# Squares of the second x tile by halves, its scaling in three pieces, the meta rows on GpSimd: the first normalization of a hybrid decoder layer

## The chip, the cores and the metric

The kernel runs on one core of one Trainium2 chip. A core has five engines, each with its own instruction queue: TensorE (PE, matrix products; PEld is its weight load), VectorE (DVE), ScalarE (ACT), GpSimd (POOL) and SyncE (SP, which here only issues DMAs). They run independently and wait for each other by semaphores. Data lie in SBUF (128 partitions) and products in PSUM, which is read by VectorE and ScalarE alone. The metric is the device time of one execution in microseconds (us), the median over several runs.

## The reference

One layer of a Hymba-like decoder on 1024 positions of width 1024, in float32, with 16 learned meta rows in front:

```python
meta = jnp.broadcast_to(meta_tokens[None].astype(x.dtype), (bsz, N_META, D_MODEL))
h = jnp.concatenate([meta, x], axis=1)
...
    u = rmsnorm(h, g_pre_mix[l])
    z = u @ w_in[l]
    q, k, v, xr, yr = jnp.split(z, split_at, axis=-1)
    attn = sliding_window_attention_with_sinks(...)
    xr = causal_depthwise_conv(xr, conv_w[l], conv_b[l])
    hr = rg_lru(xr, w_a[l], b_a[l], w_x[l], b_x[l], lru_lambda[l])
    rec = (jax.nn.gelu(yr.astype(jnp.float32)) * hr).astype(h.dtype)
    mix = jnp.concatenate([attn.astype(h.dtype), rec], axis=-1) @ w_out[l]
    h = h + rmsnorm(mix, g_post_mix[l])
    u = rmsnorm(h, g_pre_ffn[l])
    f = jnp.square(jax.nn.relu(u @ w_ff1[l])) @ w_ff2[l]
    h = h + rmsnorm(f, g_post_ffn[l])
return h[:, N_META:]
```

`rmsnorm` divides a row by the root of its mean square plus 1e-6 and multiplies it by a gain. Here only the first of these matters, `u = rmsnorm(h, g_pre_mix)`, and of it only the first 272 rows: 16 meta rows and two tiles of x with 128 rows each.

## The kernel before

Every product is made of three: each operand is split into a rounded high part and a low rest, and high*high, high*low and low*high are summed in PSUM. The high part is written by ScalarE (a copy that rounds), the low part by VectorE (a subtraction).

The beginning goes in blocks of rows: block 0 has the meta rows and x tiles 0 and 1, blocks 1 to 3 two tiles of x each. For block 0:

1. Eleven idle products (line 339) keep TensorE busy from the start while the first DMAs arrive (meta rows by ScalarE's queue; x tiles 0 and 1, the gain and the key weights by SP's).
2. Each row's sum of squares is taken: of the meta rows by ScalarE (260); of tile 0 in halves, columns 0 to 511 by ScalarE (235) and 512 to 1023 by VectorE (242, a custom instruction and the reading of its accumulator); of tile 1 by ScalarE alone (235, 1024 columns).
3. The reciprocal root: of tiles 0 and 1 by ScalarE's square root (82) and VectorE's reciprocal (195); of the meta rows by two GpSimd operations (166 and 172).
4. The rows are scaled by it on VectorE: tile 0 in two halves (248), the meta rows (266), tile 1 in two halves (248), in this order.
5. TensorE transposes them, eight column blocks kc of 128. For kc 0 to 5 (line 401) it turns all of tile 0 first, then the gain column (into a bank of its own, copied by ScalarE, 415), then the meta rows, then tile 1; kc 6 and 7 (line 426) come between the first products.
6. For each kc, ScalarE multiplies the bank by the gain and rounds it (117, the eviction), VectorE makes the low rest (118), and TensorE starts the key projection (309): first the high parts in the order of the kc, then the low ones. The products of values and queries follow, and from there TensorE has work until the end of the program.

The order on an engine is that in which a scheduler puts the code; around here it is tied by hand. `behind(name, ins)` puts an instruction after the one named, on the same engine, without a wait; `scaled[0]` holds the name of VectorE's last scaling, `last_lut[0]` of ScalarE's last table function, and `chained(0, ...)` and `chained(1, ...)` keep ScalarE's and VectorE's own chains (`last`). In `transposed_first`, `turn` chains TensorE's transposes in the order of the code.

Of the kernel before, what the change touches and what calls it, by code (L numbers as in the profile page):

```python
# [11 lines left out]
AF = mybir.ActivationFunctionType  # L12
ALU = mybir.AluOpType
# [3 lines left out]
P = 128  # L17
D = 1024
KC = D // P
T = 1024  # L20
NMETA = 16
# [6 lines left out]
EPS = 1e-6  # L28
# [9 lines left out]
def hybrid_layer(  # L38
# [6 lines left out]
    nc = tc.nc  # L45
    x, out = x[0], out[0]
# [11 lines left out]
    def slot(tag, shape, dt=F32):  # L58
        uid[0] += 1
        return slab.tile(shape, dt, tag=tag, name=f"{tag}{uid[0]}", bufs=bufs[tag])  # L60
# [4 lines left out]
    def bank(tag, shape=(P, 512)):  # L65
        uid[0] += 1
        return ps.tile(list(shape), F32, tag=tag, name=f"ps_{tag}{uid[0]}")
# [11 lines left out]
    last_lut = [None]  # L79

    def lut(*args, **kwargs):
        ins = nc.scalar.activation(*args, **kwargs).ins
        if last_lut[0] is not None:
            tc.add_manual_dep(
                ins, last_lut[0],
                mybir.DependencyInfo(
                    mybir.DependencyClass.NoSync, mybir.DependencyReason.DATA
                ),
                reason="lut",
            )  # L90
        last_lut[0] = ins.name
        return ins
# [48 lines left out]
    meta_t = slot("d", [NMETA, D])  # L141
    nc.scalar.dma_start(meta_t, meta_tokens)
    xt = []
# [19 lines left out]
    def rstd_of(ssq_parts, n=P):  # L163
        ms = small.tile([P, 1], F32, name="ms", tag="ms")
        if len(ssq_parts) == 1:
            nc.gpsimd.tensor_scalar(ms[:n], ssq_parts[0], EPS, None, op0=ALU.add)
        else:
            nc.vector.scalar_tensor_tensor(
                ms[:n], ssq_parts[0], EPS, ssq_parts[1], op0=ALU.add, op1=ALU.add
            )  # L170
        rs = small.tile([P, 1], F32, name="rs", tag="rs")
        last_pow[0] = nc.gpsimd.tensor_tensor(
            rs[:n], ms[:n], half_pow[:n], op=ALU.pow
        ).ins.name
        return rs[:n]
# [4 lines left out]
    eps_col = const.tile([P, 1], F32, name="eps_col")  # L180
# [10 lines left out]
    def root_rstd(ssq, bias, after=None):  # L191
        sd = small.tile([P, 1], F32, name="sd", tag="sd")
        lut(sd, ssq, AF.Sqrt, bias=bias)
        rs = small.tile([P, 1], F32, name="rs", tag="rs")
        ins = nc.vector.reciprocal(rs, sd).ins
        if after:
            behind(after, ins)
        return rs


    def load_cols(cols, tag="ws"):
        raw = slot("raw", [P, KC, P])
        o = 0
        for c0, n in cols:
            w, lo = c0
            nc.sync.dma_start(
                raw[:, :, o : o + n],
                w[:, lo : lo + n].rearrange("(k p) c -> p k c", p=P),
            )
            o += n  # L210
        hi, lo_ = pair(tag, [P, KC, P])
        split(hi, lo_, raw)
        return hi, lo_
# [13 lines left out]
    u = [pair("a", [P, TT]) for _ in range(KC)]  # L227
    RMS_SC = 1.0 / math.sqrt(D)

    def norm_first(src, halves):  # L230

        xn = slot("d", [P, D])
        ss = [small.tile([P, 1], F32, name=f"hq{i}", tag=f"hq{i}") for i in range(2)]
        c = slice(0, 512 if halves else D)
        square = nc.scalar.activation(
            xn[:, c], src[:, c], AF.Square, scale=RMS_SC, accum_out=ss[0]
        ).ins
        if not halves:
            behind(last_lut[0], square)
        if halves:  # L240
            c = slice(512, D)
            nc.vector.tensor_tensor_reduce(
                out=xn[:, c], in0=src[:, c], in1=src[:, c], scale=RMS_SC * RMS_SC,
                scalar=EPS, op0=ALU.mult, op1=ALU.add, accum_out=ss[1],
            )
        rs = root_rstd(ss[0], ss[1] if halves else eps_col, scaled[0])
        for c in (slice(0, 512), slice(512, D)):
            ins = nc.vector.tensor_scalar(
                xn[:, c], src[:, c], rs, None, op0=ALU.mult
            ).ins  # L250
        scaled[0] = ins.name
        return xn

    scaled = [None]


    def norm_meta():
        xn = slot("d", [P, D])
        ssq = small.tile([P, 1], F32, name="ssq", tag="ssq")
        nc.scalar.activation(  # L260
            xn[:NMETA], meta_t[:NMETA], AF.Square, scale=RMS_SC, accum_out=ssq[:NMETA]
        )
        rs = rstd_of([ssq[:NMETA]], NMETA)

        def scale():
            ins = nc.vector.tensor_scalar(
                xn[:NMETA], meta_t[:NMETA], rs, None, op0=ALU.mult
            ).ins
            behind(scaled[0], ins)
            scaled[0] = ins.name  # L270

        return xn, scale

    def norm_rows(src, link, after=None):
        xn = slot("d", [P, D])
        ssq = small.tile([P, 1], F32, name="ssq", tag="ssq")
        ins = nc.scalar.activation(
            xn, src, AF.Square, scale=RMS_SC, accum_out=ssq
        ).ins
        if link:  # L280
            chained(0, ins)
        rs = rstd_of([ssq])
        ins = [nc.vector.tensor_scalar(xn, src, rs, None, op0=ALU.mult).ins]
        if after:
            behind(after, *ins)
        elif link:
            for i in ins:
                chained(1, i)
        scaled[0] = ins[0].name
        return xn  # L290
# [57 lines left out]

    def normed(b):
        if b == 0:  # L350
            xm, scale = norm_meta()
            first = norm_first(xt[0], True)
            scale()
            return [(xm, NMETA), (first, P), (norm_first(xt[1], False), P)]
        after = mark[0]
        rows = [(norm_rows(xt[2 * b + i], b == 2, after), P) for i in range(2)]
        scaled.append(scaled[0])
        return rows


    last = [None, None]

    def chained(e, ins):
        if last[e] is not None:
            behind(last[e], ins)
        last[e] = ins.name
# [29 lines left out]
    def transposed_first(xn):  # L396
        (xm, _), (xa, _), (xb, _) = xn
        n, order = ALL[0][1], [None]

        def turn(dst, src):  # L400
            ins = nc.tensor.transpose(dst, src, ident[: src.shape[0], : src.shape[0]]).ins
            if order[0]:
                behind(order[0], ins)
            order[0] = ins.name

        def cols(kc):
            return slice(kc * P, (kc + 1) * P)

        pts = []
        for kc in range(6):  # L410
            pts.append(bank(("o", "s", "pt")[kc % 3]))
            turn(pts[kc][:, NMETA : NMETA + P], xa[:, cols(kc)])
        pg = bank("acc")
        turn(pg[:, :8], g_r)
        chained(0, nc.scalar.copy(g_mix_col, pg[:, :8]).ins)
        for kc in range(6):
            turn(pts[kc][:, :NMETA], xm[:NMETA, cols(kc)])
        for kc in range(KC):
            if kc < 6:
                pt = pts[kc]  # L420
                turn(pt[:, NMETA + P : n], xb[:, cols(kc)])
            else:
                pt = bank(("o", "s")[kc - 6])
                o = 0
                for x_, m in xn:
                    nc.tensor.transpose(pt[:, o : o + m], x_[:m, cols(kc)], ident[:m, :m])
                    o += m
            uh, ul = u[kc]
            high = split_scaled(
                uh[:, :n], ul[:, :n], pt[:, :n], g_mix_col[:, kc : kc + 1]  # L430
            )
            chained(0, high[0])
            chained(1, high[1])
            mark[0] = high[1].name
# [12 lines left out]
    def split_w(raw, tag="ws"):  # L447
        hi, lo_ = pair(tag, [P, KC, P])
        split(hi, lo_, raw)
        return hi, lo_  # L450

    xn = normed(0)
    last[0] = last_lut[0]
    rk = fetch([(K_COL, P)], pieces=2)
    rv = fetch([(V_COL, P)])
    rq = fetch([(Q_COL, HD), (Q_COL + 4 * HD, HD)], "e")
# [7 lines left out]
    last[1] = scaled[0]  # L464
    chained(1, nc.vector.tensor_copy(wk[0][:, 4:8], rk[:, 4:8]).ins)
    transposed_first(xn)
    low_w(wk, rk)
    wv = high_w(rv, "b")
# [90 lines left out]
    for b in range(4):  # L559
# [3 lines left out]
        if b == 0:  # L563
# [5 lines left out]
            xn = [(norm_rows(xt[2], True), P)]  # L569
# [29 lines left out]
    for c in range(NLRU):  # L599
# [16 lines left out]
        out=above, in_=above, pattern=[[1, P]], compare_op=ALU.is_gt, fill=0.0, base=0,  # L616
# [941 lines left out]
    halves = {}  # L1558
# [159 lines left out]
```

## Time and profile before

| | |
|---|---|
| median of 3 runs | 945.62 us (945.26 to 947.6) |
| profiled execution, its own time | 945.83 us |
| span of it, first to last instruction | 944.1 us |
| TensorE busy | 935.1 us (99%) |
| VectorE, ScalarE, GpSimd busy | 663.2, 505.8, 135.3 us |
| HBM over the span | 143 GB/s |
| granted TensorE clock, mean | 0.999 |

A row of the timeline reads: start in us from the span's beginning, duration in us, engine, line of the kernel, operation, what it writes <- what it reads (buffer numbers left out), shapes, and how many instructions the row merges; in brackets the idle time before it and what ended it. `d` are the normalized rows, `c` the loaded x tiles, `ps_o`, `ps_s`, `ps_pt` and `ps_acc` are PSUM banks, `a` the transposed and split rows, `rs` and `sd` reciprocal root and root, `hq` and `ssq` sums of squares. Instructions of an engine overlap a little, so a duration can reach past the next start. A row of the table by stretches gives, for each engine, the busy time in it and the number of its instructions. In the chain of waits each row is a piece of the path that ended last.

### The profile page before, as it was taken

The numbers are of one execution on the slowest core, as the hardware profiler recorded it, in microseconds if no ns is written. First come the engines' busy times: TensorE is split into PE (matmuls) and PEld (weight loads), VectorE is DVE, ScalarE is ACT, GpSimd is POOL, SyncE is SP. The second block draws the span as 40 slices with busy tenths as digits, with TensorE's granted clock in tenths as the row PEclk, the third lists the DMA queues.
The fourth block names the chain that finished last, engine by engine and source line by source line (L and its number), as shares of the span: only waits on it lengthen the run. The fifth ranks groups of instructions, "written<-read, shape, count | busy, mean of one in ns | idle before, by whom it ended". The sixth has DMA issues, their size and how long they took to land.

```text
span 944.1 us, 12155 instructions
## 1 busy us (share of the span) xinstructions
PE 935.1 (99%) x4562; PEld 780.9 (83%) x4562; DVE 663.2 (70%) x844; ACT 505.8 (54%) x847; POOL 135.3 (14%) x205
## 2 busy tenths in 40 slices
PE   9999999999999999999999999999999999999997
PEld 7999999877888878878888888888888888888885
DVE  7668788789877986755544465477667676779883
ACT  8546765679434854443655575653533443445441
POOL 4104437430021200110000000001121000001201
PEclk9999999999999999999999999999999999999999
DMA  8220011104359768573422374334887756637924
GB/s 274 58 67 23 24 46 45 45 23 146 100 182 290 228 193 287 181 249 129 157 89 90 115 219 119 105 112 114 199 173 173 211 180 190 192 131 208 242 63 90
DMA packets 99622, 135.96 MB, mean 144 GB/s; under 512 B 24358, under 2 KB 63286, under 8 KB 99564
## 3 DMA queue, kind: packets, MB, share of 16 engines
q1 hardware_dynamic: 90220, 109.62, 36.7%
q0 software_dynamic: 8880, 24.19, 12.3%
q10 hardware_dynamic: 464, 1.38, 0.4%
q8 instruction: 36, 0.59, 0.3%
q14 instruction: 22, 0.18, 0.1%
HBM read 113.08 MB, written 21.50 MB: 143 GB/s over the span
## 4 chain that ended last, share of the span: by engine, by line
PE 98%; DVE 1%; DMA 0%; ACT 0%; issue 0%; DVEq 0%; ACTq 0%
PE ps_acc L125 11%; PE ps_acc L130 11%; PE ps_acc L131 11%; PE ps_pt L130 7%; PE ps_pt L125 7%; PE ps_pt L131 7%; PE ps_s L125 6%; PE ps_s L131 6%; PE ps_s L130 6%; PE ps_o L125 5%; PE ps_o L130 5%; PE ps_o L131 5%; PE ps_o L763 2%; PE ps_acc L988 1%; PE ps_acc L309 1%; PE ps_s L693 1%
## 5 line engine op out<-in xcount | busy, mean ns | idle before, releaser
L99 DVE TENSOR_TENSOR ws<-raw,ws 128x1024 fp32r<-128x1024 f32 (+1 forms) x69 | 83.1, 1204 | 73.0 <-PE ps_o L130 23.0
L96 ACT CAST ws<-raw 128x1024 fp32r<-128x1024 f32 (+1 forms) x68 | 69.8, 1026 | 82.9 <-PE ps_o L130 32.8
L96 ACT CAST ws<-e 128x1024 fp32r<-128x1024 f32 x41 | 43.0, 1049 | 85.0 <-PE ps_o L130 37.8
L99 DVE TENSOR_TENSOR b<-b,b 128x1024 fp32r<-128x1024 f32 (+1 forms) x49 | 57.6, 1176 | 27.1 <-PE ps_o L130 21.9
L130 PE MATMUL ps_acc<-a,ws 128*128 128x512 f32 (+3 forms) x224 | 76.3, 341 | 0.0
L125 PE MATMUL ps_acc<-a,ws 128*128 128x512 f32 (+3 forms) x224 | 76.3, 341 | 0.0
L131 PE MATMUL ps_acc<-a,ws 128*128 128x512 f32 (+3 forms) x224 | 75.7, 338 | 0.0
L99 DVE TENSOR_TENSOR ws<-e,ws 128x1024 fp32r<-128x1024 f32 x41 | 50.1, 1223 | 31.4 <-ACT ws L96 18.0
L96 ACT CAST b<-b 128x1024 fp32r<-128x1024 f32 (+1 forms) x49 | 49.6, 1012 | 41.4 <-DVE b L1188 35.3
L750 POOL TENSOR_SCALAR_AFFINE_SELECT c<-c 128x512 fp32r<-128x512 f32 x64 | 53.1, 844 | 73.5 <-ACT c L96 64.5
L131 PE MATMUL ps_acc<-ws,b 128*128 128x512 f32 (+1 forms) x120 | 46.1, 384 | 0.0
L130 PE MATMUL ps_acc<-ws,b 128*128 128x512 f32 (+1 forms) x120 | 46.1, 384 | 0.0
L125 PE MATMUL ps_acc<-ws,b 128*128 128x512 f32 (+1 forms) x120 | 46.0, 385 | 0.0
L125 PEld LDWEIGHTS ps_acc<-a,ws 128*128 128x128 f32 x224 | 42.2, 188 | 3.1 <-DVE b L997 0.3
L131 PEld LDWEIGHTS ps_acc<-a,ws 128*128 128x128 f32 x224 | 42.2, 188 | 3.0
L130 PEld LDWEIGHTS ps_acc<-a,ws 128*128 128x128 f32 x224 | 42.1, 188 | 2.8
L125 PE MATMUL ps_pt<-ws,b 128*128 128x512 f32 x112 | 44.2, 395 | 0.0
L130 PE MATMUL ps_pt<-ws,b 128*128 128x512 f32 x112 | 44.2, 395 | 0.0
L131 PE MATMUL ps_pt<-ws,b 128*128 128x512 f32 x112 | 44.0, 393 | 0.0
L125 PE MATMUL ps_s<-ws,b 128*128 128x512 f32 x110 | 43.5, 395 | 0.0
L130 PE MATMUL ps_s<-ws,b 128*128 128x512 f32 x110 | 43.3, 393 | 0.0
L131 PE MATMUL ps_s<-ws,b 128*128 128x512 f32 x110 | 43.2, 393 | 0.0
(437 smaller groups left out, 2679.9 us busy)
## 6 DMA issues: line engine op xcount, KB each, us to landing
raw<-in_w_ff_dram SPq DMA_DIRECT2D x59, 512.0 KB
e<-in_w_ff_dram SPq DMA_DIRECT2D x43, 512.0 KB
a<-in_w_ff_dram SPq DMA_DIRECT2D x12, 512.0 KB
s_dram<-a POOLq DMA_DIRECT2D x12, 512.0 KB, 3.8
raw<-in_w_in_dram SPq DMA_DIRECT2D x9, 512.0 KB
c<-in_x_dram SPq DMA_DIRECT2D x8, 512.0 KB
d<-in_x_dram SPq DMA_DIRECT2D x8, 512.0 KB
out_dram<-raw SPq DMA_DIRECT2D x8, 512.0 KB
```

The source lines that it names most:

```text
L96: cast[0] = nc.scalar.copy(hi, src).ins.name
L99: low = nc.vector.tensor_tensor(lo, src, f32(hi), op=ALU.subtract).ins
L125: ins = nc.tensor.matmul(dst, lh, rh, start=start, stop=False, skip_group_check=True).ins
L130: nc.tensor.matmul(dst, lh, rl, start=False, stop=False, skip_group_check=True)
L131: last_mm[0] = nc.tensor.matmul(dst, ll, rh, start=False, stop=stop, skip_group_check=True).ins.name
L309: last_mm[0] = nc.tensor.matmul(acc[:, :n], w[k // 2][:, kc, :], u[kc][k % 2][:, t0 : t0 + n], start=k == 0 and kc == 0, stop=k == last an ...
L693: nc.tensor.matmul(dst, q[h][:, c], hi, start=True, stop=False, skip_group_check=True,)
L750: nc.gpsimd.affine_select(out=p_[:, :, s], in_=f32(p_[:, :, 0]), pattern=[[0, 4], [g, P]], compare_op=op, fill=0.0, base=0, channel_multip ...
L763: nc.tensor.matmul(two[:, :, oc : oc + w], v, p_.rearrange("p (j i) s c -> p j (i s c)", j=2)[:, :, pc : pc + w], start=n == 0 and k == 0, ...
L988: ins = nc.tensor.matmul(y2_bank[half], (wh, wh, wl)[k][:, kc, :], (uh, ul, uh)[k][:, t0 : t0 + n], start=m % 24 == 0, stop=m % 24 == 23, ...
```

## The change

Five things change, all in block 0:

- `norm_first` is taken apart into `squares_first` and `scale_first`. Tile 1's squares are now by halves too, ScalarE 512 columns and VectorE 512.
- VectorE's scaling of tile 0 is only its first half, and stands behind VectorE's square of tile 1.
- The second half of tile 0 is scaled by ScalarE (an ACTIVATE with Copy), behind its last square root.
- The meta rows are scaled by GpSimd, right behind their reciprocal root.
- Tile 1 is scaled in three pieces, of 256, 256 and 512 columns, and TensorE's transposes are put in another order: for kc 4 and 5 all three pieces of a bank come together, behind tile 1's first four.

```diff
-    def norm_first(src, halves):
+    def squares_first(src):
...
-        c = slice(0, 512 if halves else D)
+        c = slice(0, 512)
         square = nc.scalar.activation(
             xn[:, c], src[:, c], AF.Square, scale=RMS_SC, accum_out=ss[0]
         ).ins
-        if not halves:
+        if scaled[0]:
             behind(last_lut[0], square)
-        if halves:
...
-        rs = root_rstd(ss[0], ss[1] if halves else eps_col, scaled[0])
-        for c in (slice(0, 512), slice(512, D)):
+        c = slice(512, D)
+        ins = nc.vector.tensor_tensor_reduce(
+            out=xn[:, c], in0=src[:, c], in1=src[:, c], scale=RMS_SC * RMS_SC,
+            scalar=EPS, op0=ALU.mult, op1=ALU.add, accum_out=ss[1],
+        ).ins
+        if scaled[0]:
+            behind(scaled[0], ins)
+        scaled[0] = ins.name
+        return xn, ss
+
+    def scale_first(xn, src, rs, *cols):
+        for c in cols:
             ins = nc.vector.tensor_scalar(
                 xn[:, c], src[:, c], rs, None, op0=ALU.mult
             ).ins
-        scaled[0] = ins.name
-        return xn
+            behind(scaled[0], ins)
+            scaled[0] = ins.name
...
-        def scale():
-            ins = nc.vector.tensor_scalar(
-                xn[:NMETA], meta_t[:NMETA], rs, None, op0=ALU.mult
-            ).ins
-            behind(scaled[0], ins)
-            scaled[0] = ins.name
-
-        return xn, scale
+        nc.gpsimd.tensor_scalar(xn[:NMETA], meta_t[:NMETA], rs, None, op0=ALU.mult)
+        return xn
...
-            xm, scale = norm_meta()
-            first = norm_first(xt[0], True)
-            scale()
-            return [(xm, NMETA), (first, P), (norm_first(xt[1], False), P)]
+            xm = norm_meta()
+            xa, sa = squares_first(xt[0])
+            ra = root_rstd(*sa, scaled[0])
+            scaled[0] = roots[0]
+            xb, sb = squares_first(xt[1])
+            scale_first(xa, xt[0], ra, slice(0, 512))
+            rb = root_rstd(*sb, scaled[0])
+            scaled[0] = roots[0]
+            ins = nc.scalar.activation(
+                xa[:, 512:], xt[0][:, 512:], AF.Copy, scale=ra
+            ).ins
+            behind(last_lut[0], ins)
+            last[0] = ins.name
+            scale_first(xb, xt[1], rb, slice(0, 256), slice(256, 512), slice(512, D))
+            return [(xm, NMETA), (xa, P), (xb, P)]
...
             pts.append(bank(("o", "s", "pt")[kc % 3]))
-            turn(pts[kc][:, NMETA : NMETA + P], xa[:, cols(kc)])
+            if kc < 4:
+                turn(pts[kc][:, NMETA : NMETA + P], xa[:, cols(kc)])
...
-        for kc in range(6):
+        for kc in range(4):
             turn(pts[kc][:, :NMETA], xm[:NMETA, cols(kc)])
         for kc in range(KC):
             if kc < 6:
                 pt = pts[kc]
+                if kc > 3:
+                    turn(pt[:, NMETA : NMETA + P], xa[:, cols(kc)])
+                    turn(pt[:, :NMETA], xm[:NMETA, cols(kc)])
                 turn(pt[:, NMETA + P : n], xb[:, cols(kc)])
```

The order on the engines, as built. VectorE before, from its square of tile 0 (`c_76` is tile 0, `c_78` tile 1, `d_74` the loaded meta rows):

```order
L242 ISA d_135,hq_137<-c_76 128x512
L242 ISA hq_137 128x1
L195 RECIPROCAL rs<-sd 128x1
L248 TENSOR_SCALAR d_135<-c_76,rs 128x512 x2
L266 TENSOR_SCALAR d_128<-d_74,rs 16x1024
L195 RECIPROCAL rs<-sd 128x1
L248 TENSOR_SCALAR d_147<-c_78,rs 128x512 x2
L465 CAST b_180<-raw_157 128x512
```

And now:

```order
L243 ISA d_136,hq_138<-c_76 128x512
L243 ISA hq_138 128x1
L195 RECIPROCAL rs<-sd 128x1
L243 ISA d_145,hq_147<-c_78 128x512
L243 ISA hq_147 128x1
L254 TENSOR_SCALAR d_136<-c_76,rs 128x512
L195 RECIPROCAL rs<-sd 128x1
L254 TENSOR_SCALAR d_145<-c_78,rs 128x256 x2
L254 TENSOR_SCALAR d_145<-c_78,rs 128x512
L479 CAST b_182<-raw_159 128x512
```

The square of tile 1 has come in ahead of tile 0's scaling, of which one half is left; the meta rows are gone from this queue.

GpSimd at the same place, before:

```order
L615 AFFINE_SELECT above<-above 128x128
L166 TENSOR_SCALAR ms<-ssq 16x1
L172 TENSOR_TENSOR rs<-ms,half_pow 16x1
L653 MEMSET vmt 128x128
L166 TENSOR_SCALAR ms<-ssq 128x1
```

And now:

```order
L629 AFFINE_SELECT above<-above 128x128
L166 TENSOR_SCALAR ms<-ssq 16x1
L172 TENSOR_TENSOR rs<-ms,half_pow 16x1
L271 TENSOR_SCALAR d_128<-d_74,rs 16x1024
L667 MEMSET vmt 128x128
```

The scaling of the meta rows stands right behind their reciprocal root, ahead of the clearing of `vmt`.

TensorE before, from the gain column, which follows six transposes of tile 0, to the second of tile 1 (`d_128` are the normalized meta rows, `d_135` tile 0, `d_147` tile 1):

```order
L401 MATMUL ps_acc_196<-ident,vmt 128x8
L401 MATMUL ps_o_184<-ident,d_128 128x16
L401 MATMUL ps_s_186<-ident,d_128 128x16
L401 MATMUL ps_pt_188<-ident,d_128 128x16
L401 MATMUL ps_o_190<-ident,d_128 128x16
L401 MATMUL ps_s_192<-ident,d_128 128x16
L401 MATMUL ps_pt_194<-ident,d_128 128x16
L401 MATMUL ps_o_184<-ident,d_147 128x128
L401 MATMUL ps_s_186<-ident,d_147 128x128
```

And now, behind the gain column and four meta transposes (`d_136` is tile 0, `d_145` tile 1):

```order
L412 MATMUL ps_o_186<-ident,d_145 128x128
L412 MATMUL ps_s_188<-ident,d_145 128x128
L412 MATMUL ps_pt_190<-ident,d_145 128x128
L412 MATMUL ps_o_192<-ident,d_145 128x128
L412 MATMUL ps_s_194<-ident,d_136 128x128
L412 MATMUL ps_s_194<-ident,d_128 128x16
L412 MATMUL ps_s_194<-ident,d_145 128x128
L412 MATMUL ps_pt_195<-ident,d_136 128x128
L412 MATMUL ps_pt_195<-ident,d_128 128x16
L412 MATMUL ps_pt_195<-ident,d_145 128x128
L309 MATMUL ps_acc_264<-a_89,b_182 128x272
```

Four transposes of tile 0 and of the meta rows lead to tile 1 in place of six each; the other two banks are filled behind tile 1's first four, and the first product L309 follows them. Later, eight products of the values' low part have changed places with the first eight of the queries.

More of the change, by code (lines that the diff above doesn't have):

```diff
@@ L197, in root_rstd @@
             behind(after, ins)
+        roots[0] = ins.name
         return rs
+    roots = [None]
     def load_cols(cols, tag="ws"):
@@ L237, in norm_first @@
         ).ins
-        if not halves:
+        if scaled[0]:
             behind(last_lut[0], square)
-        if halves:
[L241 to L245, printed above, removed]
-        rs = root_rstd(ss[0], ss[1] if halves else eps_col, scaled[0])
-        for c in (slice(0, 512), slice(512, D)):
+        c = slice(512, D)
[9 more added lines that the diff above has]
+        for c in cols:
             ins = nc.vector.tensor_scalar(
@@ L452, in hybrid_layer @@
     xn = normed(0)
-    last[0] = last_lut[0]
     rk = fetch([(K_COL, P)], pieces=2)
```

## The prediction

> **What bounds the kernel now.** I read the busy shares first, then stretches of the span, then TensorE's waits, then the chain of waits around 8 us.
>
> ```profile
> PE 935.1 (99%) x4562; PEld 780.9 (83%) x4562; DVE 663.2 (70%) x844; ACT 505.8 (54%) x847; POOL 135.3 (14%) x205
> ```
> ```profile
> core 0: us, PE busy (x) PEld busy (x) DVE busy (x) ACT busy (x) POOL busy (x), PEclk, DMA share, GB/s
> 6.60:9.40 2.80, 2.34 (x19) 1.85 (x19) 2.44 (x7) 1.99 (x7) 0.20 (x1) 1.00 1.15 319
> 12.10:22.10 10.00, 10.00 (x83) 10.00 (x84) 8.36 (x13) 8.90 (x18) 5.39 (x9) 1.00 0.94 317
> 22.10:937.20 915.10, 914.99 (x4438) 763.74 (x4437) 645.12 (x807) 487.88 (x809) 124.39 (x179) 1.00 0.48 140
> ```
> ```profile
> PE ps_acc L339 <- DVE base_e L627: 1.5, 1, 1.5
> PE ps_o L401 <- DVE d L248: 0.4, 2, 0.2
> ```
> ```profile
> 6.57 0.48 DVE d L248
> 7.05 0.57 DVE d L266
> 7.62 0.16 DVE rs L195
> 7.81 0.55 DVE d L248
> 8.36 0.14 issue
> 8.49 0.31 PE ps_o L401
> 8.89 0.50 ACT a L117
> ```
>
> From 12.10 to 937.20 us TensorE is busy for 924.99 of 925.10 us, and it never waits for anything worth listing. So the body neither hides nor adds anything: when the dense products begin is carried to the end one for one. What the change touches lies before 12.1 us, where the chain runs through VectorE (second half of tile 0, meta rows, reciprocal, first half of tile 1), then the transposes of tile 1 at 8.49, then ScalarE's eight evictions (L117). That leaves about 5.5 us, between the last warm-up product near 6.58 and 12.1, in which time can be won at all; an end more than 2.8 us earlier (0.3%, about what a measurement of this kernel tells from no change) is nearly out of reach.
>
> **The squares and the first scaling.** Now ScalarE squares all of tile 1:
>
> ```profile
> 6.07 1.06 ACT L235 ACTIVATE d<-c 128x1024 f32<-128x1024 f32 x1
> 7.25 0.30 ACT L82 ACTIVATE sd<-hq,eps_col 128x1 f32<-128x1 f32 x1
> ```
> ```profile
> 4.84 0.69 DVE L242 CUSTOM_DVE_ANT_0 d<-c 128x512 f32<-128x512 f32 x1 [3.37 <-DMA c<-in_x_dram]
> 5.46 0.08 DVE L242 DVE_READ_ACCUMULATOR2_ANT hq<- 128x1 f32 x1
> 6.17 0.88 DVE L248 TENSOR_SCALAR d<-c,rs 128x512 f32<-128x512 f32 x2
> ```
>
> By halves, VectorE's square stands where the scaling of tile 0 started, at 6.17, and ends at 6.86; ScalarE's half is done by then. The root that was at 7.25 comes at about 6.96 and ends at 7.26. But the first half of tile 0, ready at 6.65 now, is queued behind that square: on VectorE alone it would end at 6.86 + 0.48 = 7.34, 0.69 later. TensorE's six transposes of tile 0 are behind it. VectorE loses 0.40 for the second half (ScalarE takes it) and 0.57 for the meta rows.
>
> **The meta rows on GpSimd** decide the price. The reciprocal root is there at 5.71 + 0.57 = 6.28; GpSimd's steps follow each other by 0.09 (5.62 to 5.71), so the scaling asks at 6.37, in the middle of VectorE's new square. What then happens is in these rows:
>
> ```profile
> 5.01 0.61 POOL L166 TENSOR_SCALAR ms<-ssq 16x1 f32<-16x1 f32 x1 [0.48 <-ACT d L260]
> 5.71 0.57 POOL L172 TENSOR_TENSOR rs<-ms,half_pow 16x1 f32<-16x1 f32 x1
> 27.02 0.22 POOL L166 TENSOR_SCALAR ms<-ssq 128x1 f32<-128x1 f32 x1 [4.41 <-ACT d L277]
> ```
> ```profile
> 202.11 0.69 DVE L917 COPY c<-c 64x1040 f32<-64x1040 f32 x1
> 202.23 1.48 POOL L916 COPY c<-c 64x1040 f32<-64x1040 f32 x1 [10.50 <-DVE c L915]
> 202.83 1.98 DVE L881 TENSOR_TENSOR b<-b,b 128x1040 fp32r<-128x1040 f32 x1
> 204.74 1.23 DVE L918 TENSOR_TENSOR c<-c,d 128x1040 f32<-128x1040 f32 x1
> ```
> ```profile
> 80.61 1.33 DVE L99 TENSOR_TENSOR ws<-raw,ws 128x1024 fp32r<-128x1024 f32 x1
> 80.82 1.61 POOL L750 TENSOR_SCALAR_AFFINE_SELECT c<-c 128x512 fp32r<-128x512 f32 x1
> 81.86 1.13 DVE L788 TENSOR_SCALAR d<-d,prm 128x1040 f32<-128x1040 f32 x1
> 27.74 0.74 DVE L283 TENSOR_SCALAR d<-c,rs 128x1024 f32<-128x1024 f32 x1
> ```
>
> The same one-column step takes 0.22 alone and 0.61 beside the square L242, ending 0.09 after it: it waited. The copy L916 ends at 203.71, 0.91 after VectorE's copy; VectorE's next operation, issued at 202.83, takes 1.98 where its sister takes 1.23, and ends 1.10 after GpSimd. At 80.82 GpSimd waits for L99, ends at 82.43, and the scaling L788 behind it needs 1.13 instead of the 0.75 of such a width, ending 0.56 after GpSimd. So the two engines exclude each other for these forms, and the one that waits goes ahead of VectorE's next instruction.
>
> Hence: GpSimd gets in at 6.86. Its 1024 columns at the copy's 0.91 per 1040 are 0.90, with the 0.09 of a scaling's start about 0.95 (an estimate): it ends at 7.81. Its bounds: 0.73, what VectorE takes for this very tile, and 1.9, twice the copy, since no GpSimd scaling of this width with a column of scalars is in the trace. I take the copy, the nearest row in shape. [...]
>
> VectorE's first half of tile 0 waits until 7.81 and then ends 0.18 sooner than its 0.48 (as L788 did, 0.56 against 0.75): 8.11. TensorE follows after 0.14, at 8.25, against 6.80 now.
>
> **TensorE's order** is then the path:
>
> ```profile
> 6.80 0.30 PE L401 MATMUL ps_o<-ident,d 128*128 128x128 f32 x1 [0.22 <-DVE d L248]
> 7.58 0.22 PE L401 MATMUL ps_acc<-ident,vmt 8*128 8x8 f32 x1
> 7.75 0.23 PE L401 MATMUL ps_o<-ident,d 16*128 16x16 f32 x1
> 8.09 0.21 PE L401 MATMUL ps_pt<-ident,d 16*128 16x16 f32 x1
> ```
>
> Six transposes took 0.78 from 6.80 to 7.58, so four take 0.56 (0.11 each); the gain column to the first meta transpose 0.17; six meta transposes span 0.34, four 0.21; another released wait 0.17, as at 7.58. So tile 1's first transpose starts at 8.25 + 0.56 + 0.17 + 0.21 + 0.17 = 9.36 instead of 8.49: **+0.87**. Its data are no hindrance: reciprocal and first quarter on VectorE follow 8.11 by 0.2 and 0.35, so by 8.7. Cutting it into 256, 256 and 512 thus wins nothing. ScalarE's scaling of tile 0's second half (about 0.6, half of L235's 1.06 and a start, at 7.2 to 7.8), the cast queued behind it and the gain column are done before 9.2, in the wait of L117 for TensorE; without that wait the 0.6 would stand in the chain. No DMA moves in any queue, and behind GpSimd's scaling only the clearing of vmt is queued, for a copy that comes much later:
>
> ```profile
> 19.88 0.21 POOL L654 COPY vmt<-c 128x16 f32<-128x16 f32 x1
> ```
>
> Behind that, two tiles' worth of transposes (kc 4 and 5) have been moved after tile 1's first four: six of 0.11 plus three satisfied waits (0.06 each) are 0.84 in place of two in 0.22, so products L309 begin some 0.6 later relative to tile 1. Most of it is hidden, since eight evictions at 0.37 set the pace; the rows of its end show how much:
>
> ```profile
> 11.11 0.27 PE L426 MATMUL ps_s<-ident,d 128*128 128x128 f32 x1
> 11.49 0.53 ACT L117 ACTIVATE a<-ps_s,gcol 128x272 fp32r<-128x272 f32 x1
> 11.70 0.77 PE L309 MATMUL ps_acc<-a,b 128*128 128x272 f32 x2
> ```
>
> The last transposes end at 11.38, 0.1 before the last eviction: no cover. The first two products waited for evictions (0.38 apart), which gives back about 0.3 of the 0.6: **+0.3** (0 if the small waits are free, 0.6 if nothing is given back). The swapped products after 14 us (values' low part ahead of the queries) wait for weights that are ready by then and cost nothing; so do VectorE's two extra instructions, whose time is in the sum.
>
> Sum: 0.87 + 0.3 = +1.2; I take +1.1, since not every released wait costs 0.17. The profiled execution took 945.83 with a span of 944.1; the median of the runs is 0.2 below it. So 945.83 + 1.1 - 0.2 = **946.7 us**, 0.1% slower and within what is told from no change.
>
> **The rivals.**
> 1. VectorE keeps its turn. Tile 0's half ends at 7.34, GpSimd gets in there, ends at 8.29, and tile 1 starts at 8.81: +0.3 + 0.3, **946.2**. Against it: both quoted precedents. Chance 0.15.
> 2. Not slower. GpSimd's 16 rows don't disturb VectorE, and released waits cost 0.11: tile 1 starts at 7.48 + 0.50 + 0.11 + 0.21 + 0.11 = 8.41, and the tail is hidden: **945.5**. It decides if GpSimd is done by 7.9. Against it: L166 with 16 rows was held up too. Chance 0.09.
> 3. GpSimd is slow or starved. At 1.9 us, or let in only after tile 1's scaling (8.5), it ends at 8.8 to 9.5; the meta transposes lead to tile 1 at 9.9 to 10.4: **947.2 to 947.8**. Chance 0.12.
> 4. The clock falls back, slower by over 0.3%:
>
> ```profile
> 1.51 5.06 PE L339 MATMUL ps_acc<-ws 128*128 128x512 f32 x11 [1.51 <-DVE base_e L627]
> 11.14 5.32 PE L309 MATMUL ps_acc<-a,b 128*128 128x272 f32 x37
> ```
>
> The warm-up products L339 take 0.46 per 512 columns, 0.9 ns a column, the products L309 0.14 per 272, 0.5 ns: TensorE starts at about half its rate and needs these 5 us to leave it (the granted clock reads 1.00 in both stretches, so the pace is the witness). Now 2.85 us pass from 6.58 to the first product at 9.43, with transposes alone; then it will be some 4 (10.7). If such a gap sends it back, 5 us of dense work run at half rate: +2.5 on top of 1.1, **949.2**. For it: the gap grows by half. Against it: 2.34 of 2.80 us of 6.60:9.40 are busy and the rate held. [...] Chance 0.10.
>
> **Numbers.** The forecast, 945.9 to 947.5 by its own bounds, has 0.54. Range for 8 in 10: **945.2 to 949.0**, from below rival 2 to just short of rival 4. Over 0.3% slower (from 948.5): rival 4 and a tail of 3, 0.13; over 0.3% faster: 0.03, for what I don't see; between: 0.84.
>
> **What would show it.** Right: GpSimd's scaling takes about 1.4 from 6.37, VectorE's first half of tile 0 shows over 1.0 instead of 0.48, tile 1's first transpose is near 9.4, the last L117 ends near 13.2. Wrong: tile 0's transposes at 7.5 (rival 1), L117 first at or before 8.9 (rival 2), GpSimd ending after 8.6 (rival 3), products L309 after 13 us more than 0.13 apart (rival 4).

## The result, and the profile after

The change is slower: 949.90 us median (949.17 to 950.74, 6 runs) against 945.66 (945.26 to 947.60, 6 runs), a ratio of 1.0045 with a 95% interval of 1.0035 to 1.0056. That is +4.24 us; the forecast was +1.1, and the time lies above the upper end of the range. The profiled execution took 949.81 with a span of 948.0 (945.83 and 944.1 before).

Stretches of the span, before and then after (columns as in the prediction; the eighth is the granted clock of TensorE):

```profile
6.60:10.00 3.40, 2.91 (x21) 2.22 (x21) 3.03 (x9) 2.59 (x8) 0.20 (x1) 1.00 1.17 313
10.00:13.40 3.40, 3.40 (x22) 2.74 (x22) 3.40 (x8) 3.40 (x8) 0.00 (x0) 1.00 0.98 329
13.40:16.80 3.40, 3.40 (x30) 3.40 (x29) 2.77 (x3) 2.98 (x6) 1.17 (x2) 1.00 0.83 195
```
```profile
6.60:10.00 3.40, 1.12 (x9) 0.87 (x9) 3.37 (x8) 1.71 (x6) 3.40 (x2) 1.00 1.19 315
10.00:13.40 3.40, 3.40 (x16) 2.37 (x14) 2.50 (x7) 2.48 (x6) 0.03 (x1) 0.50 1.07 343
13.40:16.80 3.40, 3.40 (x16) 3.12 (x16) 2.05 (x4) 2.11 (x4) 0.00 (x0) 0.50 1.10 288
16.80:26.80 10.00, 10.00 (x85) 10.00 (x85) 8.32 (x14) 8.79 (x19) 5.92 (x9) 1.00 0.72 244
26.80:941.00 914.20, 914.08 (x4434) 763.11 (x4432) 643.99 (x804) 487.02 (x807) 121.75 (x178) 1.00 0.48 140
```

From 26.8 us on nothing has changed: TensorE is busy for 914.08 of 914.20 us. Two things differ ahead of that. From 6.6 to 10.0 TensorE is busy for 1.12 us instead of 2.91. Behind that it is busy all the time, but for two stretches of 3.4 us the granted clock is 0.50, and 16 matrix operations get done where 22 and 30 did before.

Why it was idle stands in the timelines of GpSimd, VectorE, ScalarE and TensorE of the changed kernel:

```profile
6.24 3.37 POOL L271 TENSOR_SCALAR d<-d,rs 16x1024 f32<-16x1024 f32 x1
...
6.07 0.67 DVE L243 CUSTOM_DVE_ANT_0 d<-c 128x512 f32<-128x512 f32 x1
6.67 1.33 DVE L254 TENSOR_SCALAR d<-c,rs 128x512 f32<-128x512 f32 x1
8.11 1.78 DVE L254 TENSOR_SCALAR d<-c,rs 128x256 f32<-128x256 f32 x3
...
7.05 0.71 ACT L359 ACTIVATE d<-c,rs 128x512 f32<-128x512 f32 x1
10.58 0.49 ACT L117 ACTIVATE a<-ps_o,gcol 128x272 fp32r<-128x272 f32 x1 [1.45 <-PE ps_o L412]
...
8.15 0.30 PE L412 MATMUL ps_o<-ident,d 128*128 128x128 f32 x1 [1.57 <-DVE rs L195]
9.66 0.23 PE L412 MATMUL ps_o<-ident,d 16*128 16x16 f32 x1 [0.73 <-POOL d L271]
9.87 0.61 PE L412 MATMUL ps_o<-ident,d 16*128 16x16 f32 x2
10.28 0.42 PE L412 MATMUL ps_s<-ident,d 128*128 128x128 f32 x1
12.44 0.80 PE L309 MATMUL ps_acc<-a,b 128*128 128x272 f32 x2
```

GpSimd scales the meta rows until 9.61, not 7.81. TensorE has tile 0 at 8.15 (forecast 8.25), then waits 0.73 us for GpSimd and starts the meta rows at 9.66. Tile 1's first transpose is the second operation of the row at 9.87, near 10.0 (forecast 9.36); the next is at 10.28. The chain of waits says the same, GpSimd first, then transposes at half pace (start, duration):

```profile
6.24 3.38 POOL d L271
9.62 0.04 issue
9.66 0.23 PE ps_o L412
...
11.12 0.83 PE ps_s L412 x3
11.96 0.83 PE ps_pt L412 x3
12.79 0.45 PE ps_acc L309 x2
```

For comparison, the same places before:

```profile
8.49 0.30 PE L401 MATMUL ps_o<-ident,d 128*128 128x128 f32 x1 [0.20 <-DVE d L248]
8.63 0.27 PE L401 MATMUL ps_s<-ident,d 128*128 128x128 f32 x1
9.43 0.77 PE L309 MATMUL ps_acc<-a,b 128*128 128x272 f32 x2
```

So tile 1 starts 1.5 us later, and the first product 3.0 us later (12.44 against 9.43).

### The profile page after: what moved, and what is told of

The parts are those of the page before. It is cut to its first block, busy times and chain, and to the rows that moved or that the text cites. A ratio compares the mean times of both kernels' runs of the same rounds, so it can differ in the third digit from the quotient of the medians.

```text
span 948.0 us, 12158 instructions
## 1 busy us (share of the span) xinstructions
PE 937.1 (99%) x4562; PEld 783.0 (83%) x4562; DVE 664.9 (70%) x845; ACT 506.5 (53%) x848; POOL 136.6 (14%) x206
## 4 chain that ended last, share of the span: by engine, by line
PE 90%; DVE 3%; issue 2%; DMA 1%; ACT 1%; POOL 1%; DVEq 0%; ACTq 0%; POOLq 0%
PE ps_acc L125 11%; PE ps_acc L130 11%; PE ps_acc L131 11%; PE ps_s L125 6%; PE ps_s L131 6%; PE ps_s L130 6%; PE ps_pt L130 6%; PE ps_pt L125 6%; PE ps_pt L131 5%; PE ps_o L125 5%; PE ps_o L130 5%; PE ps_o L131 5%; PE ps_o L777 2%; PE ps_acc L1002 1%; PE ps_acc L309 1%
```

## The experiments

The theory at this point (T): GpSimd's scaling delays TensorE, the delay leaves TensorE without work for so long that its clock is halved, and both are paid. The rivals: the delay alone makes the whole 4.2 us; the clock falls for some other reason; the squares by halves and the new order on TensorE are what costs. Each kernel was timed beside runs of the kernel before on the same chip: those have a median of 945.47 us beside e1 to e4, 945.62 beside e7 to e10, 946.06 beside e6 and e11, 945.46 beside e13.

**e1_meta_dve: the meta rows back on VectorE.**

```diff
-        nc.gpsimd.tensor_scalar(xn[:NMETA], meta_t[:NMETA], rs, None, op0=ALU.mult)
-        return xn
+        def scale():
+            ins = nc.vector.tensor_scalar(
+                xn[:NMETA], meta_t[:NMETA], rs, None, op0=ALU.mult
+            ).ins
+            behind(scaled[0], ins)
+            scaled[0] = ins.name
+
+        return xn, scale
...
-            xm = norm_meta()
+            xm, scale = norm_meta()
...
             scale_first(xa, xt[0], ra, slice(0, 512))
+            scale()
```

> The change with one part undone: the meta rows are scaled by VectorE again, behind the first half of tile 0. Theory T (the 4.2 us are about 1.5 us of delay from GpSimd's scaling plus about 2.5 us of half clock, which follows from the delay): VectorE's square ends near 6.75, tile 0's half near 7.2, the meta rows near 7.8, tile 1's first transpose starts at 8.4 to 8.6 (before 8.49, the change 10.01), the first product L309 at 9.5 to 9.9, less than 3.4 us after the last warm-up product; granted clock 1.00 throughout: 945.5 to 946.3 us. Rival R (the squares by halves and TensorE's new order cost the time, not GpSimd): 948 us or more. A rival to the second half of T, that the clock falls for another reason than the gap: clock 0.50 in some stretch before 17 us, 948 to 949 us.

Measured: 947.61 us median, ratio 1.0012 (1.0001 to 1.0024), in two groups: five of 11 runs at 945.75 to 946.19, six at 947.61 to 951.70. The profiled one is the slowest. In it GpSimd's delay is gone:

```profile
6.80 0.48 DVE L254 TENSOR_SCALAR d<-c,rs 128x512 f32<-128x512 f32 x1
7.20 0.73 DVE L272 TENSOR_SCALAR d<-d,rs 16x1024 f32<-16x1024 f32 x1
8.05 1.01 DVE L254 TENSOR_SCALAR d<-c,rs 128x256 f32<-128x256 f32 x3
...
7.43 0.45 PE L419 MATMUL ps_o<-ident,d 128*128 128x128 f32 x1 [0.86 <-DVE d L254]
9.36 0.42 PE L419 MATMUL ps_s<-ident,d 128*128 128x128 f32 x1
11.53 0.80 PE L315 MATMUL ps_acc<-a,b 128*128 128x272 f32 x2
```
```profile
14.44:17.84 3.40, 3.40 (x17) 3.40 (x16) 3.06 (x4) 3.40 (x6) 0.08 (x1) 1.00 1.10 340
17.86:27.86 10.00, 10.00 (x86) 10.00 (x85) 7.23 (x14) 7.10 (x17) 5.16 (x9) 1.00 0.74 231
```

Tile 0's half takes 0.48 instead of 1.33, the three scalings of tile 1 take 1.01 instead of 1.78. Where the clock holds, the rest of the change costs about 0.3 us (945.8 against 945.47). But the rows of TensorE are at half pace: 0.42 for a transpose as in the change, not 0.27. In this run that is no fall of the clock: the very first transpose, at 7.43, is already slow, where the change's was still fast (0.30 at 8.15), and the pace doubles only near 17.85 (17 operations in 3.4 us, then 86 in 10). So the full clock had not come with the warm-up. The warm-up fills only part of 4.20:7.60 (2.54 us); in e7_before_idle9, below, TensorE is busy for 3.40 of the 3.40 us of 1.82:5.22, and its first transpose at 6.65 is fast (0.30). Of the other five slow runs, which have no trace, four have a mean granted clock of 0.994 or 0.995, as the change has, against 0.997 or 0.998 in the five fast ones. So T was incomplete: this kernel can go without its full clock with no GpSimd in the way, by a late rise as here, and by the means probably also by a fall.

**e2_idle18: 18 warm-up products.** The edit is `load(18, 512)` for `load(11, 512)`.

> The change with 18 warm-up products instead of 11; the added 7 lie in TensorE's wait for tile 0 and end near 8.1, before its first transpose at 8.15. Theory T (a stretch of about 3.4 us without products halves the clock for 6.8 us): the clock stays 1.00, the delay from GpSimd stays, tile 1's first transpose starts near 9.9 and the products L309 run 0.11 to 0.12 apart: 947.2 to 947.6 us, 2.3 to 2.7 below the change. Rival A (GpSimd's delay alone makes the whole 4.2 us, the clock reading is only a sign of it): 949.5 to 950. Rival B (the clock falls whatever the warm-up does, for instance by a limit on the power drawn): clock 0.50 as in the change, 949.5 to 950.

Measured: 947.54 us (947.07 to 948.85, 11 runs), 1.0022 (1.0013 to 1.0031).

```profile
6.70:10.10 3.40, 2.64 (x16) 1.74 (x15) 3.37 (x8) 1.67 (x5) 3.40 (x2) 1.00 1.16 307
10.10:13.50 3.40, 3.40 (x25) 2.64 (x25) 2.76 (x7) 2.87 (x8) 0.13 (x1) 1.00 0.99 295
```
```profile
6.34 3.46 POOL L271 TENSOR_SCALAR d<-d,rs 16x1024 f32<-16x1024 f32 x1
9.86 0.23 PE L412 MATMUL ps_o<-ident,d 16*128 16x16 f32 x1 [0.74 <-POOL d L271]
```

The first fence has the stretches, the second a row of GpSimd and of TensorE. The stretches are laid from 6.70 on, where the pace of the warm-up products doubles by an estimate: the change's start 0.42 to 0.43 apart up to 5.52 and take 0.53 each, at which pace nine would take 3.9 us, and this run's last nine, from 5.52 to 8.32, take 2.80. GpSimd is as slow as in the change, TensorE waits for it as there, and the clock stays at 1.00. That splits the 4.24 us: 2.07 (947.54 less 945.47) stay without the fall of the clock, 2.2 go with it. Both rivals, the delay alone and the clock for another reason, are out.

**e3_meta_halves: GpSimd's scaling in two instructions of 512 columns.**

```diff
-        nc.gpsimd.tensor_scalar(xn[:NMETA], meta_t[:NMETA], rs, None, op0=ALU.mult)
+        for c in (slice(0, 512), slice(512, D)):
+            nc.gpsimd.tensor_scalar(
+                xn[:NMETA, c], meta_t[:NMETA, c], rs, None, op0=ALU.mult
+            )
```

> The change with GpSimd's scaling of the meta rows as two instructions of 512 columns; TensorE's first four meta transposes need the first alone. Theory T: GpSimd's first half ends near 7.7, its second is let in behind tile 0's first half or behind a quarter of tile 1 and ends near 9.3; tile 1's first transpose starts at 9.0 to 9.3, the first product L309 at 10.9 to 11.4, over 4 us after the last warm-up product, so the clock still falls to 0.50: 948.8 to 949.4 us. If transposes alone count enough to keep the clock up to 1.5 us longer than T says: clock 1.00 and 946.5 to 947.0 us. If the two engines alternate differently and the first half also ends only behind VectorE's scalings: first meta transpose at 9.4 or later, 949.7 to 950.

Measured: 950.30 us (949.98 to 952.14, 5 runs), 1.0051 (1.0038 to 1.0063): no better than the change, and 1 us above what T said. The meta rows did come early (8.91 instead of 9.66), but at half pace this bought nothing; the mean granted clock was 0.992 or 0.993 in four of the five runs, below the change's 0.994 and 0.995. The fifth, with 0.999, is the profiled one: as in e1_meta_dve its first transpose is already slow (0.45 at 7.77), so its clock came late and didn't fall, and the run doesn't test T's gap. **e8_halves_idle18** takes the same edit with 18 warm-up products:

> The change with both remedies: GpSimd's scaling in two instructions of 512 columns, and 18 warm-up products. Theory T: clock 1.00 from 6.7 on; the warm-up ends near 8.3, TensorE's first meta transpose needs no wait (near 9.05), tile 1's first transpose starts near 9.3 (10.37 with 18 products alone), the third and fourth quarter wait for GpSimd's second half until 9.9: 946.4 to 947.0 us. If it was all the clock and GpSimd's delay costs nothing: 945.5. If splitting GpSimd's work is what made e3_meta_halves slower than the change: 948 or more.

Measured: 946.32 us (945.97 to 946.90, 11 runs), 1.0002 (0.9994 to 1.0011), 0.1 us below what T said; the meta rows start without a wait:

```profile
9.14 0.21 PE L415 MATMUL ps_o<-ident,d 16*128 16x16 f32 x1
9.63 0.27 PE L415 MATMUL ps_s<-ident,d 128*128 128x128 f32 x1
```

The second row is tile 1's second transpose, 10.28 in the change. With the clock held, GpSimd's halves give back 1.2 us of e2_idle18's time (1.4 if each is compared with the kernel before beside it: 2.07 and 0.70 above).

**e4_gpsimd_alone: the kernel before with the meta rows on GpSimd.** In `norm_meta` the line on GpSimd takes the place of `scale()`, and its call is left away.

> The kernel before with one part of the change alone: the meta rows are scaled by GpSimd; squares, scalings and TensorE's order stay as they were. Theory T: GpSimd asks at 6.3, waits for VectorE's first half of tile 0 (6.65), holds the second half until 7.6 and ends its own second turn near 8.6 to 8.8, instead of 7.62 on VectorE before; the six meta transposes start near 8.9 (before 7.75), tile 1's near 9.4 (before 8.49), the first product near 10.3, some 3.7 us after the last warm-up product: +0.9 us of delay, 946.5 us, if the clock stays; 948.8 to 949.2 if a gap of 3.7 us is enough to halve it. Rival R (squares and order cost the time): 945.5 to 946.0, the clock stays.

Measured: 949.55 us (946.73 to 950.25, 5 runs), 1.0035 (1.0021 to 1.0048); four runs at 949.27 or more with a mean granted clock of 0.992 to 0.995, one at 946.73 with 0.999, close to the 946.5 that T gave for a held clock.

```profile
6.39 3.15 POOL L265 TENSOR_SCALAR d<-d,rs 16x1024 f32<-16x1024 f32 x1
...
10.06 0.33 PE L394 MATMUL ps_o<-ident,d 128*128 128x128 f32 x1
```
```profile
6.87:10.27 3.40, 1.90 (x15) 1.40 (x16) 3.34 (x6) 1.45 (x5) 3.09 (x2) 1.00 1.21 313
10.28:13.68 3.40, 3.40 (x16) 2.81 (x14) 2.67 (x7) 2.87 (x7) 0.00 (x0) 0.50 1.00 339
```

GpSimd's scaling alone costs nearly as much as the whole change, again by both ways. T's end of GpSimd (8.6 to 8.8) was too early: 9.54.

**e7_before_idle9: the clock without any delay.** The kernel before with `load(9, 512)`.

> The kernel before, untouched but for 9 warm-up products instead of 11: they end near 5.7 instead of 6.58, nothing else is earlier or later. This tries the clock alone, without GpSimd and without any delay of the scalings. Theory T, sharpened by the first four runs (the clock is settled in stretches of about 3.41 us: full speed is granted after a stretch that products fill, and taken back after one that they leave nearly empty): the stretch that ends near 6.6 to 6.9 is no longer full, so full speed comes only at 13 us or later, or is taken back at 10; the products L309 run 0.22 apart up to there: 947.3 to 949.5 us in most runs. If the clock isn't a cause: 945.3 to 945.7, as before.

Measured: 947.39 us median (12 runs), ratio 1.0009 (0.9997 to 1.0020), in two groups again: three runs at 944.73 to 945.07, nine at 946.85 to 949.65. The interval includes no change, since the kernel before itself has 16 of 35 runs above 946.4 here. What tells them apart is the mean granted clock: 0.994 or 0.995 in six of the 12 runs, 0.996 or more in all 35 of before. The profiled run is of the second group:

```profile
5.23:8.63 3.40, 2.10 (x18) 1.53 (x17) 2.74 (x8) 2.54 (x8) 0.80 (x3) 1.00 1.08 318
8.64:12.04 3.40, 3.40 (x16) 2.68 (x14) 3.06 (x8) 2.86 (x7) 0.00 (x0) 0.50 1.17 311
```

Nothing is late in this kernel, and its clock still falls, at 8.64 in the profiled run. The stretches of 3.4 us don't end at the same time in each run, though the warm-up starts at 1.5 in both of these: here one ends at 8.63, in the change at 10.0.

**e9_meta_dve_idle14: the rest of the change, priced.** e1_meta_dve with 14 warm-up products.

> The change with the meta rows back on VectorE and 14 warm-up products, which end near 7.2 to 7.4, ahead of tile 0's first transpose. It prices the rest of the change (squares by halves, the scalings in pieces, tile 0's half on ScalarE, TensorE's order) at full clock. Theory T: full clock in all runs, tile 1's first transpose at 8.5 to 8.6, last eviction L117 starting at 11.8 to 12.0 (before 11.49) because two tiles' transposes stand between the evictions: 945.7 to 946.0 us and no run of 948 or more. Rival: e1_meta_dve's runs of 947.6 to 949.5 came from the reordering, not from the clock: the same scatter here.

Measured: 945.99 us (945.09 to 948.56, 12 runs), 1.0000 (0.9991 to 1.0010); one run above 948, which T had excluded. From its timeline:

```profile
8.58 0.27 PE L419 MATMUL ps_s<-ident,d 128*128 128x128 f32 x1
9.89 0.50 PE L315 MATMUL ps_acc<-a,b 128*128 128x272 f32 x2
```

Tile 1's second transpose, at 8.58, is as early as before (8.63), but the first product is at 9.89, 0.46 after before's 9.43: two tiles' worth of transposes have to go by first. The medians differ by 0.4 us, which the interval does not tell from nothing. The rival that squares and order cost the time is out.

**e10_transposes14: transposes in place of products.**

```diff
-    load(11, 512)
+    tail = load(11, 512)
+    for _ in range(14):
+        ins = nc.tensor.transpose(idle[:, :P], f32(zeros)[:, :P], ident).ins
+        behind(tail, ins)
+        tail = ins.name
```

> The change with 14 transposes of a zeroed tile behind its 11 warm-up products, in the place where e2_idle18 has 7 more products; they keep TensorE busy from 6.58 to about 8.1. Theory T1 (transposes don't keep the clock up): the clock falls to 0.50 near 10 us as in the change, 949.2 to 950.0 us. Theory T2 (transposes count like products; the clock fell since TensorE had next to nothing to do): clock 1.00, 947.2 to 947.6 us as with 18 products.

Measured: 947.42 us (946.61 to 951.29, 12 runs), 1.0020 (1.0009 to 1.0030): ten runs at 946.61 to 948.10 with a mean clock of 0.997 to 0.999, two above. That is the time with 18 products (947.54): in these ten, transposes held the clock as well as products. None of the 11 runs with products was above 948.85. The profiled run is one of the two above and shows where the edge lies:

```profile
5.40:8.80 3.40, 2.88 (x22) 2.29 (x21) 2.69 (x10) 2.76 (x8) 3.21 (x3) 1.00 1.14 330
8.80:12.20 3.40, 2.60 (x20) 1.92 (x19) 2.75 (x6) 1.83 (x6) 1.32 (x2) 1.00 1.15 329
12.20:15.60 3.40, 3.40 (x16) 3.12 (x16) 2.96 (x7) 2.83 (x6) 0.00 (x0) 0.50 1.13 327
```

The stretch with 2.88 us of work, which holds the 14 transposes, kept the clock; the next, behind them, with 2.60, lost it.

**e6_late3: a delay with no GpSimd in it.** The kernel before, with this ahead of tile 0's scaling:

```diff
+        if halves:
+            for _ in range(3):
+                ins = nc.vector.memset(xn[:, 0:512], 0.0).ins
+                behind(roots[0], ins)
+                roots[0] = ins.name
```

> The kernel before with three memsets of 128x512 on VectorE (0.48 us each by the row of L328) ahead of the scaling of tile 0, which overwrites them: a delay of tile 0, of the meta rows and of tile 1 by 1.3 to 1.4 us, with no GpSimd and none of the change in it. Theory T (any delay of that size leaves a stretch of 3.41 us too empty and costs the clock): tile 1's first transpose at 9.7 to 9.9, clock 0.50 for 3.4 or 6.8 us from near 10, 948.8 to 950 us in most runs. Rival (it is GpSimd's work that costs the clock or the time, not the delay as such): 946.6 to 947.0.

Measured: 949.00 us (948.96 to 950.85, 5 runs), 1.0032 (1.0020 to 1.0045).

```profile
5.41:8.81 3.40, 0.84 (x5) 0.39 (x5) 2.41 (x6) 2.44 (x7) 0.60 (x2) 1.00 1.08 317
8.82:12.22 3.40, 3.40 (x20) 3.03 (x18) 2.44 (x7) 1.01 (x4) 0.41 (x1) 0.50 1.16 284
```

All five runs have a mean granted clock of 0.992 to 0.995, the change's 0.994 and 0.995. So a delay of this size cost it with no GpSimd in it, too. The profiled run's delay was larger than meant (tile 0 at 8.65, since 0.17 us lie between the memsets).

**e12_solo: GpSimd's scaling by itself.** Added to e1_meta_dve; GpSimd's other clearing work is put behind the two measured instructions.

```diff
+    probe = slot("d", [P, D])
+    z0 = probe[:16]
+    solo = [
+        nc.vector.memset(z0, 1.0).ins,
+        nc.gpsimd.tensor_scalar(z0, z0, half_pow[:16], None, op0=ALU.mult).ins,
+        nc.gpsimd.tensor_scalar(z0[:, 0:512], z0[:, 0:512], 0.5, None, op0=ALU.mult).ins,
+    ]
```

> A measurement, on the change with the meta rows on VectorE: GpSimd also scales a spare tile of 16x1024 by a column of scalars, and then 512 columns of it by a constant, early, while VectorE has nothing to do. The predicted 0.95 us of GpSimd's scaling came from a copy at 0.91 ns a column. If that was right and the 3.37 us of the change are all waiting: 0.9 to 1.0 us for the 1024 columns. If the two holds of about 0.95 us that VectorE's rows show are GpSimd's own work: 1.8 to 2.0 us, and 0.9 to 1.0 for the 512 columns if a constant is no cheaper than a column of scalars. [...]

```profile
2.63 2.85 POOL L334 TENSOR_SCALAR d<-d,half_pow 16x1024 f32<-16x1024 f32 x1 [0.79 <-DVE base_e L656]
6.06 1.50 POOL L335 TENSOR_SCALAR d<-d 16x512 f32<-16x512 f32 x1
...
2.47 0.06 DVE L656 MEMSET base_e<- 128x4 f32 x1
5.21 0.69 DVE L243 CUSTOM_DVE_ANT_0 d<-c 128x512 f32<-128x512 f32 x1 [2.67 <-DMA c<-in_x_dram]
```

One run, used for its timeline alone: VectorE does nothing from 2.53 to 5.21, and GpSimd still needs 2.85 us for the 1024 columns; 512 columns with a constant need 1.50. Both numbers expected for the 1024 columns were too low: the prediction's 0.95 and the 1.8 to 2.0 read from VectorE's rows.

**A version that beats both was not found.** If lost clocks are also behind before's slower runs, a longer warm-up should help it. Two tries, before with `load(13, 512)` and with `load(14, 512)`:

> The kernel before with 13 warm-up products instead of 11. At full speed they end near 7.0 instead of 6.58, tile 0's transposes move by 0.2 and still end ahead of the meta rows' last transposes, so tile 1's first transpose stays at 8.49. Theory T: before's own runs of 946.4 to 948.0 us are runs in which the warm-up didn't fill a whole stretch of 3.41 us; with two more products fewer of them: median 0.2 to 0.5 us below before's in the same call, at most one run in six above 946.4. If before's scatter has nothing to do with the clock: the same median and the same share of slow runs, or 0.1 to 0.2 us more.

> The kernel before with 14 warm-up products. At half pace they last until 7.5, so that a stretch of 3.41 us full of products lies in them wherever such a stretch ends between 4.9 and 7.5 (with 11: 4.9 to 6.6; with 13: to 7.1). Where full speed comes by 6.8 they end by 7.2 and tile 1's first transpose still starts at 8.5. Theory T: at most one run in ten above 946.4 us, median 0.3 to 0.6 below before's in the same call. If e11_before_idle13's fewer slow runs were chance: the same share of them as before has in this call (7 of 15 there), and the same median or 0.1 to 0.3 more.

Measured: with 13, 945.52 us (945.05 to 947.40, 11 runs) against 946.06, 0.9993 (0.9984 to 1.0002), one run above 946.4 against seven of 15. With 14, 946.66 (945.45 to 947.84, 11 runs) against 945.46, 1.0005 (0.9993 to 1.0017), six runs above 946.4 against three of 15. The first looks like a gain, the second like a loss, and both intervals include no change. What makes before's slower runs stays open.

## Why the prediction was wrong, and what in it was right

**The step that failed first** is the price of GpSimd's scaling: "Its 1024 columns at the copy's 0.91 per 1040 are 0.90, with the 0.09 of a scaling's start about 0.95", and its upper bound of 1.9. Alone it takes 2.85 us (e12_solo). In the change GpSimd asks at 6.24, VectorE's square ends at 6.07 + 0.67 = 6.74, and 6.74 + 2.85 = 9.59, 0.02 from its end at 9.61. In e2_idle18 the same sum is 6.26 + 0.67 + 2.85 = 9.78, and it ended at 9.80. So the times fit a wait for the square, as forecast (a sum, not a row that shows the wait; in e4_gpsimd_alone, without that square, GpSimd took 3.15, 0.30 more than alone); the term was mis-sized threefold. The copy was the nearest row in width, but it was another operation.

**The second failed step** stood next to it, that a waiting VectorE gets in only when GpSimd is done. It got in between: tile 0's half ended at 8.00, 1.6 us ahead of GpSimd, and the three scalings from 8.11 were through at 9.89. They are stretched by 0.85 (1.33 against 0.48) and 0.77 (1.78 against 1.01), which together is less than GpSimd's 2.85. This error hid the first at one place: tile 0 came at 8.15, against a forecast of 8.25, for the wrong reason. The place where the true length showed is the one to which the forecast gave no wait, the meta transposes (0.73 us, to 9.66).

**The third** is the clock. It was rival 4, with a chance of 0.10, and its reason against, "2.34 of 2.80 us of 6.60:9.40 are busy and the rate held", was read from the schedule before and not redone for the one forecast. By the forecast's own times TensorE has nothing between 6.58 and 8.25; in the stretch that ended at 9.99 that would have left at most 1.7 of 3.4 us of work (an estimate from these times), and e4_gpsimd_alone lost its clock at 1.90, e7_before_idle9 at 2.10, e10_transposes14 at 2.60. So even with a GpSimd as fast as assumed, rival 4 was probably the likelier end (no run has the delay that was forecast). Its price came out well, +2.5 forecast and 2.2 measured, but partly by luck: it was worked out for 5 us of dense products at half rate, and the change has 6.8 us at half rate, the first half of them mostly transposes. Rival 3, a slow GpSimd, was put at 947.2 to 947.8, and e2_idle18, which is that case with the clock held, has 947.54. The two were taken for alternatives, though the first brings about the second.

Whether a transpose counts for the clock like a product has two sides here. For keeping it, no run shows a difference: ten of the 12 runs of e10_transposes14 kept it with transposes (mean clock 0.997 to 0.999), as e2_idle18 did with products (0.997 to 0.999). For getting it back, two traces look as if transposes did less. In the change 10.00:13.40 is filled without a gap (3.40 of 3.40), mostly by transposes, and the next stretch is still at 0.50; only after that one, in which the products L309 come in, is the clock back. In e6_late3 8.82:12.22 was full of transposes likewise, and there the next stretch, 12.24:15.64, with transposes still standing between the products, didn't bring it back either: 15.65:19.05 has 0.50 too. How much a transpose counts was not measured by itself.

**Right:** that the body passes a shift on unchanged; that GpSimd waits for VectorE's square (by the sums above); that ScalarE's half of tile 0 (7.05 to 7.76) disappears in its wait of 1.45 us before the first eviction L117; that cutting tile 1's scaling in three wins nothing (in the change TensorE waits for GpSimd; no run leaves the cut out); and the +0.3 for the tail, in whose place e9_meta_dve_idle14 has 0.46 at the first product and 0.4 in the time (not told from zero). The sum as measured: 0.37 for the rest (945.99 of e9_meta_dve_idle14 less 945.62), 1.70 for GpSimd (2.07 of e2_idle18 less 0.37), and what is left of the 4.24, 2.17, for the clock; forecast were 0.3, 0.9 and 0.

## What to carry to other kernels

Before work is moved to an engine on which no trace shows that operation, measure it alone, in a place where the other engines are idle: a row of nearly the same width and another operation was wrong by a factor of three (0.95 against 2.85). And where TensorE gets its speed from a warm-up, as here (a transpose took 0.42 us ahead of the full clock in e1_meta_dve and 0.27 with it in the change; the clock was settled in stretches of 3.4 us), count the work that it will have in each such stretch of the new schedule up to the first dense products, not of the old one; a gap was paid twice here, once as delay (1.70 us) and once as pace (2.17). The clock was repaired by cheap products in the gap (mean 0.997 to 0.999 in e2_idle18 and e8_halves_idle18), the delay was not (2.07 us left in e2_idle18).

## What was not expected of the hardware

- GpSimd needs 2.85 us to scale 16x1024 by a column of scalars and 1.50 for 16x512 by a constant, some 2.8 to 2.9 ns a column, three times the 0.9 that the prediction worked out for a copy.
- VectorE's scalings got through while one GpSimd scaling ran (in the change from 6.24 to 9.61). They were held up by 0.85 and 0.77 us, not for its length.
- The clock was settled in stretches of 3.4 us: it fell at 10.0 in the change, 10.28 in e4_gpsimd_alone, 8.64 in e7_before_idle9, 12.20 in e10_transposes14, 8.82 in e6_late3, and then ran at 0.50 for one such stretch (e10_transposes14), two (the change, e4_gpsimd_alone, e7_before_idle9) or three (e6_late3). It fell after stretches with 0.84 to 2.60 us of work and held after 2.64 (e2_idle18, its stretch laid by the estimate above) and more. In the change the 0.50 lasts from 9.99 to 16.82, 6.83 us, or two times 3.41. That such stretches lie differently in the executions of one program, and make the two groups of times of e1_meta_dve and e7_before_idle9, is argued, not shown: one run of each has a trace.
- In e1_meta_dve's profile the granted clock reads 1.00 from 7.61 to 14.43 while a transpose takes 0.42 us as at 0.50; e3_meta_halves, at a mean of 0.999, is alike. In these two the column shows nothing of the late rise; the pace does.
